# A transformer block in fp32: x also comes transposed from the host, and w_in's columns lie in the order of use

## The chip, the core and the metric

The kernel runs on one core of a Trainium2 chip. The metric is the device time of one execution in microseconds, as the median of several runs. The profile is of one execution, with the times of each engine's instructions: PE (TensorE, matmuls; PEld is its weight load), DVE (VectorE), ACT (ScalarE), POOL (GpSimd) and SP (SyncE, which here only issues DMAs). L361 means line 361 of the kernel.

## The reference, cut to what matters

One residual block on x of 256 tokens by 2048 channels, all in float32. A combined projection w_in (2048 x 5120) gives q, k and v of four attention heads and the two halves of a gated convolution branch; both results go through w_out, and a SwiGLU of width 5632 follows.

```python
xn = rms_norm(h, norm1_g[l])
proj = jnp.einsum('bsd,dn->bsn', xn, w_in[l].astype(xn.dtype))
q, k, v, ga, gg = jnp.split(proj, ..., axis=-1)
...
u = ga * jax.nn.sigmoid(gg)
u = causal_depthwise_conv(u, conv_w[l], conv_b[l])
u = jax.nn.silu(layer_norm(u, conv_ln_g[l], conv_ln_b[l]))
mixed = jnp.concatenate([att, u], axis=-1)
h = h + jnp.einsum('bsm,md->bsd', mixed, w_out[l].astype(mixed.dtype))
...
h = h + jnp.einsum('bsf,fd->bsd', jax.nn.silu(a) * bu, w_down[l].astype(hn.dtype))
```

## The kernel before, in words

**Products in three parts.** Each fp32 operand is split into a rounded part (hi) and the rest (lo), both in the fast fp32r format. A product is the sum of three matmuls: x_hi with w_hi (L361), x_lo with w_hi (L362) and x_hi with w_lo (L367). x is the stationary operand, a k-tile of 128 channels by 128 tokens; 512 columns of weights stream through. Each k-tile is therefore used in six matmuls, three for each of the two halves of the tokens.

**Chunks.** A matrix is worked off in blocks of 512 output columns, a block in chunks of two k-tiles, so that a chunk has 12 matmuls. `load_chunk` (L307) issues the chunk's weights on SP's DMA queue into one of five raw buffers (from the second block on, every third chunk goes to one of two spare buffers). `round_chunk` (L320) makes w_hi with a cast on ACT, L322. `split_chunk` (L328) makes w_lo with a subtraction on DVE, L331. `multiply` (L343) does the matmuls, first all with w_hi, then those with w_lo. `run_chunks` (L389) writes all of this down in one order: load, cast and split run ahead of the matmuls by one chunk in the opening (the first eight chunks) and by two after it. Each engine works through its instructions in that order.

**Steps beside the chunks.** Everything else is a generator that is resumed twice in each chunk, once between the two halves of the matmuls and once behind them (`resume`, L246). A `yield` puts the next step half a chunk later. The order on each engine is thus fixed by counts of chunks, not by time. The convolution's 240 taps on DVE (L512) are dealt out by a credit per k-tile (`run_side`, L272).

**The order of the work.** w_in comes first, in ten blocks: four for the convolution (each 256 columns of the gate and 256 of the value, thus two DMAs of 256 KB for a chunk), then k and q for two heads at a time, then v. Then come w_out, the gate and up matrices, and the down matrix. A block's sums lie in two PSUM banks, of four, until its finishing generator has read them: `glu_done` (L478) for the convolution, `qk_done` and `v_done` for the attention. `conv_back` (L526) takes the finished convolution through a layer norm: it transposes y to tokens (ps_y), makes its statistics on DVE (L543, L552) and POOL, normalises on ACT (L561), transposes back (ps_ln, L570), applies SiLU (z, L574) and splits into mchi and mclo (L577, L578), the operand of w_out's k-tiles 8 to 15.

**The opening before.** x comes with tokens on the partitions, in five pieces, each as two DMAs into the two tiles h (`x_load`, L432). Its k-tiles are transposed on PE (ps_x, L441), 32 transposes in all, and split from PSUM by ACT and DVE, scaled by the gain of the norm (`split_scaled`, L232; L235 and L236). The norm's factor rstd1 is applied to the block's sums later; its sum of squares comes from eight squares with an accumulated sum on ACT (L430), two reductions on DVE and four small POOL operations (L215). The gains come as rows and are transposed on PE (L157), and so are the convolution's weights (eight transposes, L184). 14 transposes of the identity at the start and five behind the first pieces of x keep PE busy (`warm_up`, L142).

Of the kernel before, what the change touches and what calls it, by code (L numbers as in the profile page):

```python
# [56 lines left out]
CONV_BLOCKS = (2, 2, 2, 2)  # L57
# [51 lines left out]

@with_exitstack  # L110
def tile_block(
    ctx: ExitStack,
    tc: tile.TileContext,
    x, w_in, conv_w, w_out, w_gate, w_up, w_down, gains, vecs, rope, out,
# [27 lines left out]
    def warm_up(n):  # L142
        warm = aux_ps.tile([P, N], F32, tag="aux", name="ps_warm")
        for _ in range(n):
            pe.transpose(warm[:, :P], ident, ident)

    warm_up(WARM[0])

    rows = pre.tile([NR, P], F32, tag="rows", name="rows", bufs=1)
    act.dma_start(out=rows, in_=gains)  # L150

    act.copy(small.tile([P, 8], F32, tag="rsq", name="first"), neghalf)
    cols = const.tile([P, NR], F32, tag="cols", name="cols")

    def gain_columns():
        ps = aux_ps.tile([P, N], F32, tag="aux", name="ps_cols")
        pe.transpose(ps[:, :NR], rows, ident[:NR, :NR])  # L157
        act.copy(cols, ps[:, :NR])
# [7 lines left out]
    cw_rows = [pre.tile([W, N], F32, tag="va", name="cw_rows") for _ in range(CC // N)]  # L166
# [4 lines left out]
    def late_loads():  # L171
        flat = conv_w.rearrange("o w i c -> (o w i) c")
        for i in range(CC // N):
            sp.dma_start(out=cw_rows[i], in_=flat[:, i * N : (i + 1) * N])
        for t, v in ((gb, vecs[:2]), (lamv, vecs[2:])):
            sp.dma_start(out=t, in_=v.rearrange("(o v) d -> o v d", o=1).to_broadcast(list(t.shape)))
        sp.dma_start(out=rt, in_=rope.rearrange("(m p) c d -> p m c d", p=P))

    def late_constants():
        late_loads()  # L180
        yield from lag(4)
        pw = aux_ps.tile([P, N], F32, tag="aux", name="ps_cw")
        for ct in range(NCT):
            pe.transpose(pw[:, ct * W : (ct + 1) * W], cw_rows[ct * P // N][:, ct * P % N : ct * P % N + P], ident[:W, :W])  # L184
        act.copy(cw.rearrange("p c w -> p (c w)"), pw[:, : NCT * W])
# [57 lines left out]
    def start(gen):  # L243
        running.append(gen)
# [45 lines left out]
    def block(w, cols, ks, xs, done=None, bkey=None, first=True, last=True, spare=False, cuts=()):  # L290
# [7 lines left out]
        while i < len(ks):  # L298
            part = ks[i : i + (cuts.pop(0) if cuts else NK * N // width)]
            i += len(part)  # L300
            chunks.append(dict(w=w, k0=part[0], nk=len(part), cols=cols, width=width, xs=xs, bkey=bkey,
# [124 lines left out]
    ss1 = [small.tile([P, D // N], F32, tag=f"ss1_{m}", name=f"ss1_{m}", bufs=1) for m in range(NM)]  # L426
# [4 lines left out]

    def x_load(ks):  # L432
        cs = slice(ks[0] * P, (ks[-1] + 1) * P)
        for m in range(NM):
            sp.dma_start(out=h[m][:, cs], in_=x[m * P : (m + 1) * P, cs])

    def x_part(ks):
        for k in ks:
            ps = aux_ps.tile([P, N], F32, tag="aux", name="ps_x")
            for m in range(NM):  # L440
                pe.transpose(ps[:, m * P : (m + 1) * P], h[m][:, k * P : (k + 1) * P], ident)  # L441
            xT[k] = lhs_pair("x", k)
            split_scaled(xT[k], ps[:, :S], col("g1", k))

    def x_rest():
        c = 0
        for part in XPARTS[1:]:
            while chunks_done[0] < (part[0] // NK) * 2 - 1:
                yield
            x_part(part)  # L450
            yield
            yield
            if part[-1] % (N // P) == N // P - 1:
                for m in range(NM):
                    square_sum(h[m][:, c * N : (c + 1) * N], ss1[m][:, c : c + 1])
                c += 1
        for m in range(NM):
            ss = small.tile([P, 1], F32, tag="ss1", name="ss1")
            dve.tensor_reduce(ss, ss1[m], AX.X, ALU.add)
            rsqrt_mean(rstd1[m], ss, D, EPS)  # L460
        yield
        normed.append(True)
# [122 lines left out]
    qkT = {key: pre.tile([P, 2 * H, S], F32, tag=f"{key}T", name=f"{key}T", bufs=1) for key in "qk"}  # L585

# [581 lines left out]
    QC, KC, VC, AC, GC = 0, 1024, 2048, 3072, 4096  # L1168
    fx, fh = xT.get, hT.get
    fm = lambda k: mixa.get(k) if k < 8 else mixc.get(k - 8)  # L1170
    c0 = 0
    for nct in CONV_BLOCKS:
        block(w_in, [(GC + c0 * P, nct * P), (AC + c0 * P, nct * P)], range(KD), fx,
              lambda ps, c0=c0, nct=nct: glu_done(c0, nct, ps))
        c0 += nct
    for b in range(2):
        block(w_in, KC + b * N, range(KD), fx, lambda ps, b=b: qk_done("k", b, ps))
        block(w_in, QC + b * N, range(KD), fx, lambda ps, b=b: qk_done("q", b, ps))
    for b in range(2):
        block(w_in, VC + b * N, range(KD), fx, lambda ps, b=b: v_done(b, ps))  # L1180
# [22 lines left out]
    for part in XPARTS:  # L1203
        before[part[0] // NK] = lambda part=part: x_load(part)
# [5 lines left out]
_FLAT = {"x": (S, D), "w_in": (D, 5120), "conv_w": (1, W, 1, CC), "w_out": (D, D), "w_gate": (D, FF),  # L1210
# [22 lines left out]
```

## Time and profile before

| | us |
|---|---|
| median of 3 runs (lowest to highest) | 1051.15 (1050.9 to 1052.19) |
| span of the profiled execution, first to last instruction | 1049.4 |
| PE busy in it | 1040.1 |
| DVE busy in it | 896.4 |
| ACT busy in it | 622.1 |

The profile gives the span of the profiled execution and no other time of that execution; the median of the runs lies 1.75 us above the span. The rows that the next part shows come from five views. The page's head has the busy time of each engine and its share of the span. A row of the stretches gives, for a window in us, the length, then for PE, PEld, DVE, ACT and POOL the busy time and the number of instructions, then the granted clock, the mean busy share of the 16 DMA engines and their GB/s. A row in order of time gives start and duration in us (of several instructions in a row, from the first's start to the last's end), engine, line, operation, what is written and read, and in brackets the engine's idle time before it and what ended that. The DMA view has one figure of GB/s for each fortieth of its window, and for an issue its size and the time to landing. The view of a tile sums up its instructions and the waits ahead of them.

### The profile page before, as it was taken

The numbers are of one execution on the slowest core, as the hardware profiler recorded it, in microseconds if no ns is written. First come the engines' busy times: TensorE is split into PE (matmuls) and PEld (weight loads), VectorE is DVE, ScalarE is ACT, GpSimd is POOL, SyncE is SP. The second block draws the span as 40 slices with busy tenths as digits, with TensorE's granted clock in tenths as the row PEclk, the third lists the DMA queues.
The fourth block names the chain that finished last, engine by engine and source line by source line (L and its number), as shares of the span: only waits on it lengthen the run. The fifth ranks groups of instructions, "written<-read, shape, count | busy, mean of one in ns | idle before, by whom it ended". The sixth has DMA issues, their size and how long they took to land.

```text
span 1049.4 us, 13104 instructions
## 1 busy us (share of the span) xinstructions
PE 1040.1 (99%) x4702; PEld 855.9 (82%) x4702; DVE 896.4 (85%) x1091; ACT 622.1 (59%) x798; POOL 99.3 (9%) x143
## 2 busy tenths in 40 slices
PE   8999999999999999999999999999999999999998
PEld 7888888877888788888888888888888888888886
DVE  4799989899675599999788898989978699989897
ACT  6645567756666565776453557666654447657442
POOL 0030022201100100000001000001000110010010
PEclk9999999999999999999999999999999999999999
DMA  9755555544446565988766789879757789798682
GB/s 297 238 180 199 186 176 180 176 158 148 168 155 231 190 233 204 260 271 255 217 224 175 226 262 272 254 217 292 244 182 240 201 221 290 222 290 263 187 266 86
DMA packets 122893, 229.22 MB, mean 218 GB/s; under 512 B 7892, under 2 KB 25742, under 8 KB 122828
## 3 DMA queue, kind: packets, MB, share of 16 engines
q1 hardware_dynamic: 113904, 201.61, 56.5%
q0 software_dynamic: 8864, 26.74, 13.3%
q8 instruction: 37, 0.61, 0.2%
q14 instruction: 28, 0.23, 0.1%
q10 hardware_dynamic: 60, 0.03, 0.0%
HBM read 202.14 MB, written 9.44 MB: 202 GB/s over the span
## 4 chain that ended last, share of the span: by engine, by line
PE 62%; DVE 2%; DMA 1%; ACT 0%; issue 0%; DVEq 0%
PE q L1017 12%; PE q L1011 12%; PE q L1012 12%; PE q L992 8%; PE q L990 8%; PE q L991 8%; PE ps_a L828 1%; DMA raw<-in_w_down_dram 1%; PE acc L367 1%; PE acc L361 1%; PE acc L362 1%; DVE wlo L331 1%; DVE wlt L973 0%; DVE wt L963 0%; ACT wh L969 0%
## 5 line engine op out<-in xcount | busy, mean ns | idle before, releaser
L322 ACT CAST whi<-raw 128x1024 fp32r<-128x1024 f32 x272 | 281.5, 1050 | 145.8 <-PE acc L362 56.8
L331 DVE TENSOR_TENSOR wlo<-raw,whi 128x1024 fp32r<-128x1024 f32 x238 | 288.3, 1224 | 82.2 <-ACT whi L322 82.1
L969 ACT CAST wh<-wt 128x2048 fp32r<-128x2048 f32 x52 | 99.5, 1914 | 78.7 <-DVE wt L965 78.3
L973 DVE TENSOR_TENSOR wlt<-wt,wh 128x2048 fp32r<-128x2048 f32 x52 | 119.1, 2290 | 14.7 <-ACT wh L969 14.5
L361 PE MATMUL acc<-whi,xhi 128*128 128x512 f32 x320 | 126.3, 395 | 1.0 <-ACT whi L322 0.9
L362 PE MATMUL acc<-whi,xlo 128*128 128x512 f32 x320 | 125.0, 391 | 0.5 <-DVE xlo L236 0.5
L1011 PE MATMUL q<-whi,chi 128*128 128x512 f32 x320 | 125.2, 391 | 0.0
L1012 PE MATMUL q<-whi,clo 128*128 128x512 f32 x320 | 124.6, 389 | 0.0
L990 PE MATMUL q<-wh,fhi 128*128 128x512 f32 x280 | 109.8, 392 | 0.0
L991 PE MATMUL q<-wh,flo 128*128 128x512 f32 x280 | 109.0, 389 | 0.0
L512 DVE SCALAR_TENSOR_TENSOR y<-upad,cw,y 128x256 f32<-128x256 f32 x240 | 102.5, 486 | 0.0
L1011 PE MATMUL q<-whi,ahi 128*128 128x512 f32 x256 | 100.2, 391 | 0.0
L1012 PE MATMUL q<-whi,alo 128*128 128x512 f32 x256 | 99.6, 389 | 0.0
L972 DVE TENSOR_TENSOR wlb<-wb,wh 128x1536 fp32r<-128x1536 f32 x52 | 91.1, 1752 | 1.8 <-ACT wh L966 1.8
L367 PE MATMUL acc<-wlo,xhi 128*128 128x512 f32 x320 | 87.7, 396 | 0.9 <-DVE wlo L331 0.8
L1017 PE MATMUL q<-wlo,chi 128*128 128x512 f32 x320 | 85.8, 390 | 0.0
L966 ACT CAST wh<-wb 128x1536 fp32r<-128x1536 f32 x52 | 76.7, 1474 | 0.0
L361 PEld LDWEIGHTS acc<-whi,xhi 128*128 128x128 f32 x320 | 60.1, 188 | 13.9 <-ACT whi L322 1.2
L362 PEld LDWEIGHTS acc<-whi,xlo 128*128 128x128 f32 x320 | 60.1, 188 | 13.5 <-DVE xlo L236 1.3
L1017 PEld LDWEIGHTS q<-wlo,chi 128*128 128x128 f32 x320 | 59.9, 188 | 13.1 <-DMA wlo<-raw 0.7
L367 PEld LDWEIGHTS acc<-wlo,xhi 128*128 128x128 f32 x320 | 59.3, 188 | 13.6 <-DVE wlo L331 1.8
L1012 PEld LDWEIGHTS q<-whi,clo 128*128 128x128 f32 x320 | 60.1, 188 | 12.3
(229 smaller groups left out, 1744.6 us busy)
## 6 DMA issues: line engine op xcount, KB each, us to landing
raw<-in_w_down_dram SPq DMA_DIRECT2D x64, 512.0 KB, 7.5
raw<-in_w_in_dram SPq DMA_DIRECT2D x48, 512.0 KB, 4.4
raw<-in_w_gate_dram SPq DMA_DIRECT2D x48, 512.0 KB, 6.9
raw<-in_w_up_dram SPq DMA_DIRECT2D x48, 512.0 KB, 6.2
wb<-in_w_up_dram SPq DMA_DIRECT2D x40, 512.0 KB, 3.8
wb<-in_w_gate_dram SPq DMA_DIRECT2D x40, 512.0 KB, 4.7
wlo<-raw POOLq DMA_DIRECT2D x34, 512.0 KB, 6.8
raw<-in_w_in_dram SPq DMA_DIRECT2D x64, 256.0 KB, 5.7
```

What stands on the lines that cost most here:

```text
L322: act.copy(c["hi"], c["raw"])
L331: dve.tensor_tensor(c["lo"], c["raw"], c["hi"].bitcast(F32), ALU.subtract)
L361: pe.matmul(ps[m], xhi[:, ms], hi[:, j, :], start=c["first"] and j == 0, stop=False)
L362: pe.matmul(ps[m], xlo[:, ms], hi[:, j, :], start=False, stop=False)
L367: pe.matmul(ps[m], xhi[:, ms], lo[:, j, :], start=False, stop=c["last"] and j == nk - 1)
L512: dve.scalar_tensor_tensor(y[:, ct, :], src, wk, y[:, ct, :], ALU.mult, ALU.add)
L973: dve.tensor_tensor(lot, c["t"], c["hi"][:, :SUMMED].bitcast(F32), ALU.subtract)
L990: pe.matmul(ps, hi, c["hi"][:, w], start=bool(first), stop=False)
L991: pe.matmul(ps, lo, c["hi"][:, w], start=False, stop=False)
L1011: pe.matmul(ps, xs[i][0][:, ms], hi[:, i, :], start=i == 0 and bool(c["first"].get(qs[m])), stop=False)
L1012: pe.matmul(ps, xs[i][1][:, ms], hi[:, i, :], start=False, stop=False)
L1017: pe.matmul(sum_bank(c, qs[m]), xs[i][0][:, ms], lo[:, i, :], start=False, stop=i == 1 and bool(c["last"].get(qs[m])))
```

## The change

- The host passes x a second time, transposed: `xt`, 128 channels by 16 k-tiles by 256 tokens. `x_load` brings it in five pieces (one, three, and three times four k-tiles), one DMA each, into the tiles that later hold q and k. `x_split` splits the k-tiles from SBUF; the 32 transposes go.
- The host orders w_in's columns as the blocks use them, so that every chunk is one DMA of 512 columns. It passes the gains as columns and the convolution's weights as 128 channels by 248, so that those nine transposes go too.
- The first two chunks of the first block have one k-tile each (256 KB of weights, six matmuls), so that the block has nine chunks, and the opening lasts nine.
- The sum of squares is made from the transposed x: four squares in place on ACT (128x1024), five additions on DVE, and two matmuls with a column of -0.5 for the sum over the channels (`x_norm`).
- Token-major x is loaded into h as two DMAs of 1 MB ahead of the load of chunk 40 (`x_whole`). It is wanted for the residual, behind w_out.
- The identity is transposed 17 times at the start, and no more after that.

```diff
-WARM = (14, 5)
-XPARTS = (range(0, 2), range(2, 4), range(4, 8), range(8, 12), range(12, 16))
-OPENING = KD // NK
+WARM = 17
+XLOADS = {0: range(0, 1), 1: range(1, 4), 3: range(4, 8), 5: range(8, 12), 7: range(12, 16)}
+XSQUARES = 4
+XWHOLE = 40
+FIRST_CUTS = (1, 1)
+OPENING = KD // NK + 1
...
+def w_in_columns():
+    q, k, v, a, g = (np.arange(1024) + 1024 * i for i in range(5))
+    c = CONV_TILES * P
+    conv = [part[i : i + c] for i in range(0, CC, c) for part in (g, a)]
+    return np.concatenate([*conv, k[:N], q[:N], k[N:], q[N:], v])
...
     def x_load(ks):
-        cs = slice(ks[0] * P, (ks[-1] + 1) * P)
-        for m in range(NM):
-            sp.dma_start(out=h[m][:, cs], in_=x[m * P : (m + 1) * P, cs])
-
-    def x_part(ks):
+        half = qkT["qk"[ks[0] // 8]]
+        sp.dma_start(out=half[:, ks[0] % 8 : ks[-1] % 8 + 1, :], in_=xt[:, ks[0] : ks[-1] + 1, :])
+
+    def x_split(ks):
         for k in ks:
-            ps = aux_ps.tile([P, N], F32, tag="aux", name="ps_x")
-            for m in range(NM):
-                pe.transpose(ps[:, m * P : (m + 1) * P], h[m][:, k * P : (k + 1) * P], ident)
             xT[k] = lhs_pair("x", k)
-            split_scaled(xT[k], ps[:, :S], col("g1", k))
+            split_scaled(xT[k], qkT["qk"[k // 8]][:, k % 8, :], col("g1", k))
...
+    def x_square(n):
+        part = lambda i: qkT["qk"[i // 2]][:, i % 2 * XSQUARES : (i % 2 + 1) * XSQUARES, :]
+        act.activation(part(n), part(n), AF.Square)
+        if n:
+            dve.tensor_tensor(part(0), part(0), part(n), ALU.add)
+
+    def x_norm():
+        for n in range(KD // XSQUARES):
+            while len(xT) < (n + 1) * XSQUARES:
                 yield
-            x_part(part)
-            yield
-            yield
...
+            x_square(n)
+            yield
+        sq = qkT["q"]
+        for w in (2, 1):
+            dve.tensor_tensor(sq[:, :w, :], sq[:, :w, :], sq[:, w : 2 * w, :], ALU.add)
+        yield from lag(2)
+        yield from room(1)
+        ps = aux_ps.tile([P, N], F32, tag="aux", name="ps_n")
+        for m in range(NM):
+            pe.matmul(ps[:, m : m + 1], sq[:, 0, m * P : (m + 1) * P], neghalf[:, :1], start=True, stop=True)
+        yield
+        ss = small.tile([P, NM], F32, tag="ss1", name="ss1")
+        act.copy(ss, ps[:, :NM])
+        for m in range(NM):
+            rsqrt_mean(rstd1[m], ss[:, m : m + 1], -D / 2, EPS)
         yield
         normed.append(True)
...
-    before[0] = lambda: (x_load(XPARTS[0]), gain_columns(), x_part(XPARTS[0]), warm_up(WARM[1]), start(x_rest()))
+    def opening(i):
+        def begin():
+            if i in XLOADS:
+                x_load(XLOADS[i])
+            x_split(chunks[i]["ks"])
+            if not i:
+                start(x_norm())
+        return begin
+
+    def x_whole():
+        for m in range(NM):
+            sp.dma_start(out=h[m], in_=x[m * P : (m + 1) * P, :])
+
+    for i in range(OPENING):
+        before[i] = opening(i)
     before[OPENING] = lambda: start(late_constants())
+    before[XWHOLE] = x_whole
```

More of the change, by code (lines that the diff above doesn't have):

```diff
@@ L113, in tile_block @@
     tc: tile.TileContext,
[L114 removed]
+    x, xt, w_in, conv_w, w_out, w_gate, w_up, w_down, gains, vecs, rope, out,
 ):
@@ L145, in warm_up @@
             pe.transpose(warm[:, :P], ident, ident)
-    warm_up(WARM[0])
-    rows = pre.tile([NR, P], F32, tag="rows", name="rows", bufs=1)
-    act.dma_start(out=rows, in_=gains)
+    warm_up(WARM)
+    cols = const.tile([P, NR], F32, tag="cols", name="cols")
+    act.dma_start(out=cols, in_=gains)
     act.copy(small.tile([P, 8], F32, tag="rsq", name="first"), neghalf)
[L153 to L158, printed above, removed]
     def col(key, k):
@@ L180, in late_constants @@
         late_loads()
[L181 to L185, printed above, removed]
         while not normed:
```

54 lines of the change are left out of this document (18 added, 36 removed).

## The prediction, made before the changed kernel ran

> **What bounds the kernel now.** I read the page first, then the stretches of the opening, the waits of the first 60 us, and the opening and the middle in order of time.
>
> ```profile
> span 1049.4 us, 13104 instructions
> PE 1040.1 (99%) x4702; PEld 855.9 (82%) x4702; DVE 896.4 (85%) x1091; ACT 622.1 (59%) x798; POOL 99.3 (9%) x143
> ```
> ```profile
> 5.00:10.00 5.00, 4.08 (x22) 3.44 (x22) 2.10 (x3) 2.99 (x6) 0.00 (x0) 1.00 0.88 261
> 10.00:15.00 5.00, 4.49 (x24) 3.45 (x23) 3.24 (x4) 3.06 (x9) 0.00 (x0) 1.00 1.07 368
> 15.00:20.00 5.00, 4.92 (x21) 3.49 (x20) 3.08 (x6) 4.75 (x11) 0.00 (x0) 1.00 1.08 359
> 60.00:80.00 20.00, 20.00 (x92) 16.58 (x91) 20.00 (x35) 9.77 (x15) 8.58 (x14) 1.00 0.60 184
> ```
> PE (first busy figure of a stretch) is the bound nearly everywhere. So a change pays only by taking instructions from PE or by filling PE's holes, and the holes lie before 20 us. The last two figures say why: from 10 to 20 us the DMA engines are full (1.07, 368 GB/s), while at 60 us they are 0.60 busy.
>
> ```profile
> 1.35 3.25 PE L145 MATMUL ps_warm<-ident 128*128 128x128 f32 x14 [1.35 <-POOL neghalf L139]
> 5.72 0.83 PE L145 MATMUL ps_warm<-ident 128*128 128x128 f32 x5
> 6.38 1.04 ACT L322 CAST whi<-raw 128x1024 fp32r<-128x1024 f32 x1
> 7.48 0.50 PE L361 MATMUL acc<-whi,xhi 128*128 128x512 f32 x1 [0.93 <-ACT whi L322]
> 8.05 0.40 PE L361 MATMUL acc<-whi,xhi 128*128 128x512 f32 x1
> 9.21 0.40 PE L362 MATMUL acc<-whi,xlo 128*128 128x512 f32 x1
> 12.65 1.05 ACT L322 CAST whi<-raw 128x1024 fp32r<-128x1024 f32 x1 [1.91 <-DMA raw<-in_w_in_dram]
> 22.24 0.39 PE L361 MATMUL acc<-whi,xhi 128*128 128x512 f32 x1
> 24.96 0.39 PE L361 MATMUL acc<-whi,xhi 128*128 128x512 f32 x1
> 26.78 1.03 PE L441 MATMUL ps_x<-ident,h 128*128 128x128 f32 x8
> 34.02 0.39 PE L361 MATMUL acc<-whi,xhi 128*128 128x512 f32 x1
> ```
> The real work starts at 7.48. A chunk (two k-tiles, 12 matmuls) without additions takes 24.96 - 22.24 = 2.72 us. The first block has eight chunks, 21.8 us of matmuls, and the second block starts at 34.02: 26.5 us after the first matmul. The 4.8 us over are the transposes of x within the block (28 of them, at 1.03/8 = 0.13 us at most 3.6 us) and waits (1.2 us or more).
>
> **The change, part by part.**
>
> *The opening.* What arrives when, by one row (GB/s in slices of 1 us from 0 to 40):
>
> ```profile
> GB/s 0 29 243 270 333 195 226 343 254 289 360 377 364 381 357 348 356 368 370 353 348 356 311 302 291 331 226 305 183 151 56 327 337 276 287 300 330 339 366 348
> raw<-in_w_in_dram SPq DMA_DIRECT2D x38, 256.0 KB, 5.8
> ```
> Before, the first cast needs two k-tiles of x and of weights, 768 KB, which the running sum of the row reaches at 4.7 us; the cast starts at 6.38, so landing and semaphore add 1.65 us. After, the first cast needs 128 KB of x and 256 KB of weights: reached at 3.45, cast at 5.1. For a 128x512 cast I take 0.62 us, just above the 0.59 of the ACT copy of that size below. First matmul: 5.7 us instead of 7.48. The 17 transposes in a row end earlier: 3.25 us for 14, so 3.9 us for 17, done at 5.3.
>
> ```profile
> 40.97 0.59 ACT L501 COPY upad<-ps_u 128x512 f32<-128x512 f32 x1 [1.25 <-PE ps_u L500]
> 27.20 1.57 ACT L235 ACTIVATE xhi<-ps_x,cols 128x256 fp32r<-128x256 f32 x4 [1.51 <-PE ps_x L441]
> 27.71 1.66 DVE L236 SCALAR_TENSOR_TENSOR xlo<-ps_x,cols,xhi 128x256 fp32r<-128x256 f32 x4 [0.76 <-ACT xhi L235]
> 29.74 1.23 DVE L331 TENSOR_TENSOR wlo<-raw,whi 128x1024 fp32r<-128x1024 f32 x1 [0.37 <-ACT whi L322]
> ```
> Chunks 0 and 1 (one k-tile, 1.36 us each) and chunk 2 could be done at 5.7 + 5.44 = 11.15. The next one (k-tiles 4 and 5) decides. Ahead of its cast stand 2560 KB, exactly what stood ahead of the cast at 12.65 before; by that pace its first matmul comes at 12.65 + 1.05 + 0.05 = 13.75. The other end is 11.15, with PE alone. Between them stands ACT: the weights of chunk 2 (1536 KB so far) land at 8.3 by the best pace of the row (370 kB per us) with the 1.65 us behind it, and at 9.4 by the old pace. Then follow a cast of 1.05, the new squares of four k-tiles (128x1024; I take the cast of that size, 1.05), two x casts (0.8) and a cast of 1.05: 12.3 to 13.4. I take 12.6, nearer the fast end: a load of a conv chunk is now one DMA of 512 KB and not two of 256 KB, so whatever number of DMAs is in flight carries more bytes, and at 5 to 7 us the row dips to 195 and 226 though more loads were ready to go.
>
> From there six chunks of 2.72 lead to the second block: 12.6 + 16.3 = 28.9, against 34.02. **Term A: -5.1 us**, ends -6.6 (PE alone, 27.45) and -3.95 (old pace, 30.05). It contains the 28 transposes, the stalls and the earlier start. DVE must keep up: from 12.4 us on it has six wlo (1.23), five pairs of x splits (0.83), three new sums of 128x1024 (1.23), and two short ones (some 1.1 together): 7.4 + 4.2 + 3.7 + 1.1 = 16.4 us, done at 28.8. That is just in time for the two norm matmuls, which stand at 28.9; this cover has nothing to spare. Splitting from SBUF instead of PSUM I cost at 0: the duration could only differ by part of a 0.42 us instruction.
>
> *Gains and conv weights.* Both now come in the order in which they are used.
>
> ```profile
> 4.53 0.36 PE L157 MATMUL ps_cols<-ident,rows 58*128 58x58 f32 x1
> 38.64 0.68 PE L184 MATMUL ps_cw<-ident,cw_rows 31*128 31x31 f32 x8
> ```
> The gain transpose lay ahead of the first matmul (in A). The eight conv transposes stood in PE's full stream: **B: -0.7 us**. The Trainium skill (DMA: Bandwidth & Descriptors, Specifications) asks for at least 512 B per piece; the gains' rows are now 232 B. Before, the gains were there by 4.53 without a wait of PE, and no row prices such short ones.
>
> *The norm.* Two fp32 matmuls with one column replace nothing on PE: between nothing and the 0.36 us of the 58-column one, each. **C: +0.35 us** for both (0.1 to 0.7). The eight squares and reads on ACT and two reductions on DVE go; four squares and five sums come, counted above. rstd1 is ready two to three chunks later than before, but the sums of a block stay in one of two pairs of PSUM banks until the next block but one starts, eight chunks on.
>
> *The conv branch.* This is the cost I would not have seen in the diff. Block one has nine chunks, and the norm's steps are tied to chunks, so the first taps stand half a chunk to a chunk later in the order on DVE, and so does everything behind the last tap. In the built order of PE, the transposes of y for the second half move from matmul 1044 to 1052, and those of the normalised y from 1092, 1100, 1104, 1112 to 1100, 1104, 1112, 1116 (counted in 512-column matmuls). The w_out matmuls that read the result stay at 1104. Before, this chain had little slack:
>
> ```profile
> 280.06 0.33 DVE L552 BATCH_NORM_AGGREGATE mv<-stats 128x2 f32<-128x12 f32 x2
> 282.80 0.19 POOL L557 TENSOR_SCALAR lnb<-lnb 128x2 f32<-128x2 f32 x1
> 285.39 1.52 ACT L561 ACTIVATE upad<-upad,lnb,lnr 128x512 f32<-128x512 f32 x2
> 286.82 1.00 ACT L574 ACTIVATE z<-ps_ln,cols 128x256 f32<-128x256 f32 x2
> 287.72 0.43 DVE L578 TENSOR_TENSOR mclo<-z,mchi 128x256 fp32r<-128x256 f32 x1
> 288.79 1.23 DVE L331 TENSOR_TENSOR wlo<-raw,whi 128x1024 fp32r<-128x1024 f32 x1
> 289.78 0.40 PE L362 MATMUL acc<-whi,mclo 128*128 128x512 f32 x1
> ```
> mclo is done at 288.15 and first read at 289.78: 1.6 us to spare. After, the aggregate stands behind one more weight split and ends 1.85 us later against PE's stream; z stands behind the same casts, and one wlo (1.23, of which 0.8 counts) comes ahead of mchi on DVE: mclo is some 2.75 us later, while PE arrives 0.4 us earlier, since one group of transposes now stands behind these matmuls. 2.75 + 0.4 - 1.6: **D: +1.5 us**, ends 0 (the 1.6 us of slack plus the two POOL steps running shorter) and 2.4.
>
> *Token-major x at chunk 40.* 2 MB more on SP's queue between two weight loads.
>
> ```profile
> DMA to landing us min/median/max: 3.6/4.5/5.9
>   PE acc L362: 15.9, 10
> ```
> This is the view of the weight loads from 95 to 130 us: they land at most 5.9 us after the issue, and the casts wait for PE (10 times) and never for a DMA. Of seven raw buffers, a load goes out some four to five chunks before its cast, 11 to 13.6 us. The 2 MB take 2.1/0.37 = 5.7 us, less than what is left, and the cast itself runs two chunks ahead of its matmuls. Cost 0; without that cover see below. The 2 MB are wanted only by the residual, after 290 us.
>
> **Sum:** -5.1 - 0.7 + 0.35 + 1.5 = -3.95 us. The profiled span of 1049.4 becomes 1045.45. The median of the runs lies 1.75 us above that span; I leave this as it is: 1051.15 - 3.95 = **1047.2 us**.
>
> **The rivals.**
> 1. *More is won:* the loads keep up (A -6.3) and the conv chain fits (D 0): 1044.9. For it: fewer, larger DMAs; against it: ACT's chain above.
> 2. *The feed stays as slow as before*, so the earlier start turns into waits for DMA: A is -3.95, 1048.4. This is also how the small first chunks would fail to do what they are for: at 12.65 the old kernel had received just as many bytes. Against it: the DMA engines were not full from 5 to 10 us (0.88).
> 3. *The clock.* The 14 transposes run at 0.23 us each, the later ones at 0.13, and the first real matmuls already at their full pace (8.05 to 9.21 is five, 0.23 each). So PE's pace doubled within the second group of transposes, some 4.6 us after its first instruction, though the granted clock of the stretches stands at 1.00. If the longer gap without real matmuls, or transposes alone, do not bring that about, the first matmuls run at half pace for 4.6 us: of 24 matmuls in chunks 0 to 2 some 10 are done at 10.3, the rest at 13.5, 0.9 us behind 12.6: 1048.1. The Trainium skill (TensorE: Matmul & The Clock Gate, Part 4: PE-mode transpose) says that transposes do not count as busy for the clock; by that rule this case would hold. The trace disagrees: the pace doubled with nothing but transposes issued.
> 4. *Slower than before:* the 2 MB of x hold up the weights. If the loads behind them land later than their casts are due and the two chunks of lead are used up, PE stands for as long as x takes: at 300 kB per us, 7 us, giving 1054.2. It decides once the delay exceeds the 5 to 8 us left before the cast and the 4 us after it. Against it: DMA is 0.60 busy there.
>
> **How the numbers follow.** The forecast has 0.55, rival 1 0.18, rival 2 0.12, rival 3 0.05, rival 4 0.06; 0.04 is left for an opening on DVE that does not fit. The range joins the ends: -6.6 - 0.7 + 0.1 + 0 = -7.2 gives 1044.0; -3.95 - 0.6 + 0.7 + 2.4 = -1.45 gives 1049.7. A measurement of this kernel can tell some 0.2%, 2.1 us, from no change: faster means below 1049.05. The forecast and rivals 1 to 3 lie there but for their upper ends: faster 0.85, same 0.08, slower 0.07.
>
> **What would show it.** First matmul at 5.7 (5.2 to 6.5), the first of chunk 3 near 12.6, the second block at 28.9. No wait of the norm matmuls over 0.3 us. One wait of PE for mclo or mchi of 1 to 2 us where w_out's second half starts, 4 us earlier than 289. No wait of a cast for a DMA around 100 to 125 us. I am wrong if the second block starts after 31 us, or if stalls that the change does not touch (the attention between 210 and 265 us) move by more than 1 us.

## The result, and the profile after

| | before | after |
|---|---|---|
| median of 14 runs each, us | 1051.12 (1050.71 to 1052.41) | 1049.12 (1048.44 to 1049.90) |
| span of the profiled execution, us | 1049.4 | 1047.1 |

The ratio is 0.9979, 95% interval 0.9971 to 0.9987: 2.0 us faster, and inside the range that was given (1044.0 to 1049.7). The interval excludes 1, but the prediction called a result faster only below 1049.05, and 1049.12 is just above that line. The forecast was 1047.2; half of the gain that it counted on did not arrive. The opening won nearly what it should. Some 2.3 us were taken back in three places behind it, of which the prediction had named one.

The page of the changed kernel, and its stretches (length; busy time and count of PE, PEld, DVE, ACT, POOL; granted clock; DMA share; GB/s):

```profile
span 1047.1 us, 12933 instructions
PE 1036.2 (99%) x4663; PEld 852.5 (81%) x4663; DVE 900.6 (86%) x1095; ACT 621.6 (59%) x786; POOL 100.5 (10%) x143
...
5.00:10.00 5.00, 4.05 (x14) 2.74 (x12) 2.32 (x5) 2.71 (x5) 0.00 (x0) 1.00 0.93 337
10.00:15.00 5.00, 4.91 (x22) 3.94 (x22) 4.20 (x7) 4.67 (x9) 0.00 (x0) 1.00 1.05 399
15.00:20.00 5.00, 5.00 (x24) 4.14 (x23) 5.00 (x8) 4.51 (x7) 0.00 (x0) 1.00 1.05 392
```

PE has 39 instructions fewer. The feed from 5 to 20 us is faster than before (337, 399 and 392 GB/s against 261, 368 and 359), and from 15 us on PE is busy without a hole. The opening in order of time, changed kernel:

```profile
1.36 3.89 PE L157 MATMUL ps_warm<-ident 128*128 128x128 f32 x17 [1.36 <-POOL neghalf L151]
4.89 0.78 PE L359 MATMUL acc<-whi,xhi 128*128 128x512 f32 x1
5.47 0.63 PE L360 MATMUL acc<-whi,xlo 128*128 128x512 f32 x1
5.89 0.63 PE L359 MATMUL acc<-whi,xhi 128*128 128x512 f32 x1
...
7.16 0.51 ACT L233 ACTIVATE xhi<-qT,cols 128x256 fp32r<-128x256 f32 x1 [2.54 <-DMA qT<-in_xt_dram]
8.47 0.50 PE L359 MATMUL acc<-whi,xhi 128*128 128x512 f32 x1 [0.95 <-ACT whi L320]
...
13.06 0.39 PE L359 MATMUL acc<-whi,xhi 128*128 128x512 f32 x1
...
29.39 0.50 PE L460 MATMUL ps_n<-neghalf,qT 128*128 128x1 f32 x4
29.75 0.49 PE L359 MATMUL acc<-whi,xhi 128*128 128x512 f32 x1
```

The first matmul comes at 4.89, but the second chunk stands until 8.47: ACT waits until 7.16 for the piece of x with k-tiles 1 to 3, and its cast of the second chunk's weights stands behind that. Chunk 3 (k-tiles 4 and 5) starts at 13.06, and from there six chunks run at 2.72 us each up to the norm's matmuls at 29.39, which wait for nothing and take 0.36 us (29.75 - 29.39).

Where the lead goes is seen by setting the same work side by side. Counted are the 512-column matmuls of the blocks, in groups of twelve; the table has the start of a group in both traces.

| start of | before | after | lead |
|---|---|---|---|
| first matmul | 7.48 | 4.89 | 2.59 |
| group 8 (second block) | 34.02 | 29.75 | 4.27 |
| group 11 | 43.54 | 38.52 | 5.02 |
| group 55 (q and k) | 166.82 | 161.85 | 4.97 |
| group 56 | 170.03 | 166.14 | 3.89 |
| group 72 | 220.42 | 216.78 | 3.64 |
| group 90 (w_out) | 282.74 | 279.12 | 3.62 |
| group 93 | 292.77 | 290.11 | 2.66 |
| end of the span | 1049.4 | 1047.1 | 2.3 |

So 1.08 us are lost within one group of q and k, 0.25 in two groups near 214 us, 0.96 where w_out's second half begins, and 0.36 behind it. The first of these, in the changed kernel (POOL, DVE, ACT and PE in order of time):

```profile
143.11 1.09 ACT L543 COPY upad<-ps_y 128x512 f32<-128x512 f32 x2
...
148.00 0.42 POOL L217 TENSOR_SCALAR rsq<-ssq 128x4 f32<-128x4 f32 x1 [19.74 <-ACT junk L427]
148.50 3.40 POOL L218 TENSOR_TENSOR fq<-rsq,neghalf 128x4 f32<-128x4 f32 x1
148.68 2.35 DVE L329 TENSOR_TENSOR wlo<-raw,whi 128x1024 fp32r<-128x1024 f32 x2
152.31 1.14 ACT L619 ACTIVATE qn<-acc,fq 128x128 f32<-128x128 f32 x4 [1.61 <-POOL fq L615]
154.42 1.23 DVE L329 TENSOR_TENSOR wlo<-raw,whi 128x1024 fp32r<-128x1024 f32 x1 [3.39 <-ACT whi L320]
...
164.74 1.20 PE L365 MATMUL acc<-wlo,xhi 128*128 128x512 f32 x4 [0.80 <-DVE wlo L329]
```

and the same chain before:

```profile
152.39 0.19 POOL L219 TENSOR_SCALAR rsq<-ssq 128x4 f32<-128x4 f32 x1 [19.16 <-ACT junk L430]
...
154.08 2.23 POOL L612 TENSOR_SCALAR fq<-fq,rstd 128x4 f32<-128x4 f32 x1
156.34 1.14 ACT L616 ACTIVATE qn<-acc,fq 128x128 f32<-128x128 f32 x4 [1.26 <-POOL fq L612]
```

Before, ACT starts qn when the factors fq are there, at 156.34, which less the lead of 4.97 is 151.37; after, at 152.31. It is 0.94 us late, ACT's next weight casts stand behind it, DVE idles for 3.39 us (2.28 before), and ten microseconds later PE waits for a wlo. A POOL step on four columns that takes 3.40 us is the odd row here, but it is not the larger part. POOL has such a row in both traces (3.40 after, 2.23 before), and its steps up to fq take 4.28 us after (148.00 to 152.28) and 3.92 before (152.39 to 156.31): 0.36 us more. The other 0.58 us are there when POOL starts (148.00, against 152.39 - 4.97 = 147.42), because ACT's squares end later: the two copies of ps_y at 143.11 now stand directly ahead of two weight casts and the squares, while before they stood at 144.95, ahead of 1.58 us in which ACT was idle. On DVE one tap more (0.39 us) stands ahead of the wlo for which PE waits. The three add up to the 1.33 us by which that wlo is late against the lead (its subtraction starts at 163.47, before at 167.11 - 4.97 = 162.14). That the order of the steps is behind them is shown by e1 and e2.

The third loss, at w_out's second half in the changed kernel:

```profile
279.71 1.07 POOL L562 TENSOR_SCALAR lnb<-lnb 128x2 f32<-128x2 f32 x1
280.81 2.94 ACT L566 ACTIVATE upad<-upad,lnb,lnr 128x512 f32<-128x512 f32 x4 [1.34 <-POOL lnb L562]
...
286.20 0.50 PE L359 MATMUL acc<-whi,mchi 128*128 128x512 f32 x1 [0.58 <-DVE mchi L582]
```

This is the wait for mchi that the prediction named; the first matmul with mclo follows 0.46 us later. Before, the same POOL step took 0.19 us, but there the first step of the same chain took 1.20 us.

### The profile page after: what moved, and what is told of

It is laid out like the page before. It is cut to its first block, busy times and chain, and to the rows that moved or that the text cites. A ratio compares the mean times of both kernels' runs of the same rounds, so it can differ in the third digit from the quotient of the medians.

```text
span 1047.1 us, 12933 instructions
## 1 busy us (share of the span) xinstructions
PE 1036.2 (99%) x4663; PEld 852.5 (81%) x4663; DVE 900.6 (86%) x1095; ACT 621.6 (59%) x786; POOL 100.5 (10%) x143
## 4 chain that ended last, share of the span: by engine, by line
PE 61%; DMA 2%; DVE 2%; issue 1%; ACT 0%; DVEq 0%; POOLq 0%
PE q L1020 12%; PE q L1014 12%; PE q L1015 12%; PE q L995 8%; PE q L993 7%; PE q L994 7%; DMA raw<-in_w_down_dram 1%; PE ps_a L831 1%; DMA wlo<-raw 1%; PE acc L365 1%; PE acc L359 1%; PE acc L360 1%; DVE wlo L329 1%; DVE wlt L976 0%; DVE wt L966 0%
## 5 line engine op out<-in xcount | busy, mean ns | idle before, releaser
L320 ACT CAST whi<-raw 128x1024 fp32r<-128x1024 f32 (+1 forms) x273 | 281.5, 1048 | 141.6 <-PE acc L360 58.9
L329 DVE TENSOR_TENSOR wlo<-raw,whi 128x1024 fp32r<-128x1024 f32 (+1 forms) x239 | 287.8, 1218 | 73.5 <-ACT whi L320 73.3
L1014 PEld LDWEIGHTS q<-whi,chi 128*128 128x128 f32 x320 | 60.1, 188 | 12.3
```

The source lines that it names most:

```text
L320: act.copy(c["hi"], c["raw"])
L329: dve.tensor_tensor(c["lo"], c["raw"], c["hi"].bitcast(F32), ALU.subtract)
L1014: pe.matmul(ps, xs[i][0][:, ms], hi[:, i, :], start=i == 0 and bool(c["first"].get(qs[m])), stop=False)
```

## The experiments

The theory at this point: the opening won about 5 us; the conv chain standing half a chunk to a chunk later on DVE makes all three later waits. The rivals: the opening is held by the size of x's pieces, or the later waits have another cause. Of the numbers below, "opening" means the start of the matmuls of k-tiles 4 and 5 and of the second block. Every run was timed beside the kernel before; ratios are to it. None of the twelve kernels leaves out any part of the computation.

**e1: the norm half a chunk earlier** (in `x_norm` of the changed kernel)

```diff
-        yield from lag(2)
+        yield from lag(1)
```

> The changed kernel with the norm's two matmuls half a chunk earlier (one resume less of waiting in x_norm). In the built order this puts the first taps, the y transposes and the transposes of the normalised y back at the places they had in the old kernel (120, 564 and 1044, 1092 to 1112). If the order is what costs the changed kernel its time behind the opening (theory: order), the wait of PE for wlo at 163.6 us (1.0 us) and the one for mchi at 286.2 (0.6, with mclo some 1.0) go, and nothing else moves: the span falls from 1047.1 by 2.0 to 1045.1, the median to about 1047.0, ratio to the old kernel 0.996. If the two waits are chance, of POOL and DVE running in another phase after the shorter opening (theory: phase), the first one stays and the ratio is 0.997 or above. The norm matmuls then stand at about 28.5 us, the sums on DVE are done at 28.6: a wait of at most 0.3 us.

Measured: 1047.62 us (5 runs), ratio 0.9967 (0.9954 to 0.9979). The wait at 163.6 and those for mchi and mclo are gone. But two new ones stand in the second block (view in order of time, e1):

```profile
28.49 0.58 PE L460 MATMUL ps_n<-neghalf,qT 128*128 128x1 f32 x4
...
36.17 0.94 PE L505 MATMUL ps_u<-ident,u 128*128 128x128 f32 x4 [0.61 <-DVE u L497]
```

PE now reaches the transposes of u 0.6 us before DVE has made u, and the norm's matmuls stand in the middle of a chunk, ahead of its wlo. So the order decides, as the theory has it (it said 1047.0). Pulling the whole of it forward costs 1.18 us of lead in the second block (3.84 at group 11, against 5.02), half of the 2.29 us that it saves later.

**e2: the kernel before, with the norm's end delayed by as much**

```diff
         yield
+        yield from lag(4)
         normed.append(True)
```

> The old kernel with four resumes more before the norm counts as done, which puts the first taps and all that follows at the places of the changed kernel (128, 572 and 1052, 1100 to 1116) and leaves the opening as it was. Theory order: it becomes slower by the 2.0 us that the changed kernel loses behind its opening, median 1053.1, ratio 1.002, with a wait for wlo some 4 us later than 163.6 and one for mchi. Theory phase: no change but the second wait at most, ratio 1.000 to 1.001.

Measured: 1053.82 us (8 runs), ratio 1.0024 (1.0013 to 1.0034). The old kernel, with its old opening and x transposed on the chip, now has the same waits, in the same places and of the same size (PE in order of time, e2):

```profile
169.97 1.19 PE L367 MATMUL acc<-wlo,xhi 128*128 128x512 f32 x4 [0.79 <-DVE wlo L331]
...
291.39 0.49 PE L361 MATMUL acc<-whi,mchi 128*128 128x512 f32 x1 [0.58 <-DVE mchi L578]
```

The two idle times of the changed kernel were 0.80 and 0.58. Counted by the same groups, e2 falls behind the kernel before by 1.04, 0.27 and 0.97 us, where the changed kernel lost 1.08, 0.25 and 0.96. That the three losses come from the shifted order, and not from x, w_in or the loads, is shown by this run together with e1.

**e3: k-tile 1 of x by itself**

```diff
-XLOADS = {0: range(0, 1), 1: range(1, 4), 3: range(4, 8), 5: range(8, 12), 7: range(12, 16)}
+XLOADS = {0: range(0, 1), 1: range(1, 2), 2: range(2, 4), 3: range(4, 8), 5: range(8, 12), 7: range(12, 16)}
```

> The changed kernel with x in six loads: k-tile 1 alone ahead of the weights of chunk 1, k-tiles 2 and 3 behind them. In the changed kernel chunk 1 waits 1.3 us for the load of k-tiles 1 to 3 (384 KB, landed at 7.1), and runs at 8.47. Theory feed: 256 KB less stand ahead of it, so chunk 1 starts 0.7 to 1.0 us earlier, and so does all that follows: second block at 29.0 instead of 29.75, ratio 0.9972. Theory ACT: chunk 2 is set by the cast of its weights and the splits on ACT, chunk 1 starts earlier and the second block does not: ratio 0.998 as before.

Measured: 1048.72 us (11 runs), ratio 0.9979 (0.9970 to 0.9988), that of the changed kernel. The second chunk no longer waits for x (it starts at 6.75 instead of 8.47), and nothing comes of it. ACT and PE in order of time, e3:

```profile
8.65 1.04 ACT L320 CAST whi<-raw 128x1024 fp32r<-128x1024 f32 x1 [0.75 <-DMA raw<-in_w_in_dram]
11.90 1.05 ACT L320 CAST whi<-raw 128x1024 fp32r<-128x1024 f32 x1 [0.45 <-PE acc L360]
13.00 0.50 PE L359 MATMUL acc<-whi,xhi 128*128 128x512 f32 x1 [0.22 <-ACT whi L320]
```

ACT's wait moved on to the weights of the next chunk, and then to a whi buffer that PE had not yet freed; k-tiles 4 and 5 start at 13.00. The time in which the second chunk stands in the changed kernel lies beside loads and casts that set the start of chunk 3 anyway.

**e4: the kernel before, with w_in's columns in the order of use**

```diff
-        block(w_in, [(GC + c0 * P, nct * P), (AC + c0 * P, nct * P)], range(KD), fx,
+        block(w_in, c0 // 2 * N, range(KD), fx,
...
+    given["w_in"] = given["w_in"][:, w_in_columns()]
```

> The old kernel with w_in's columns in the order of use alone: each chunk is one DMA of 512 KB with rows of 2 KB instead of two of 256 KB with rows of 1 KB. Theory feed: the opening was held up by the loads (casts waited 6.2 us for them), so the waits of PE within the first block (1.2 us or more) and part of the wait ahead of it shrink: second block 1 to 1.5 us earlier than 34.02, ratio 0.9988. Theory transposes: what the change gained in the opening was the transposes and the smaller first chunks, and the feed matters little: ratio 0.9995 to 1.

Measured: 1051.04 us (11 runs), ratio 1.0002 (0.9993 to 1.0011). The first matmul comes later and the second block when it did (PE in order of time, e4; 34.02 before):

```profile
8.34 0.50 PE L369 MATMUL acc<-whi,xhi 128*128 128x512 f32 x1 [1.35 <-ACT whi L330]
...
33.91 0.39 PE L369 MATMUL acc<-whi,xhi 128*128 128x512 f32 x1
```

With the transposes still in the stream, larger loads alone win nothing.

**e5: only the first taps half a chunk earlier**

```diff
         act.copy(upad[c0 // NB][:, c0 % NB : c0 % NB + nct, W - 1 :], pt[:, :nct])
-        yield
+        if c0:
+            yield
```

> The changed kernel with one difference: for the first block's conv chunk the pause between copying u into upad and starting the taps is dropped, so that the norm and the transposes of u stay where the change put them (96 and 128 in 512-column matmuls) while the taps, and the transposes of y (564, 1044) and of the normalised y (1092, 1100, 1104, 1112) behind them, go back to the old places. Nothing is left out. Theory (the later order of the taps alone makes the late waits): the waits at 163.6 us (1.19), at the start of w_out's second half (0.85 and 0.46) and the 0.4 more at 214 go, and the waits at ps_n and ps_u that the kernel with the norm moved had (0.49 and 1.00) do not come: 2.3 us below the changed kernel, 1046.8 us, ratio about 0.996. Rival (the late waits come from where the norm stands, not from the taps): they stay, 1049.1, ratio 0.998. Rival (the time given back comes out elsewhere, as with the moved norm): 1047.7.

Measured: 1047.46 us (5 runs), ratio 0.9961 (0.9949 to 0.9974). The waits for mchi and mclo are gone, as in e1, and the new waits of e1 do not come. But a wait near 164 is still there (1.39 us of lead go between groups 53 and 56), and the time lies between the theory's 1046.8 and the 1047.7 of time given back: the place of the taps alone does not explain this wait, and the theory falls for it. In order of time, e5:

```profile
149.68 3.49 DVE L329 TENSOR_TENSOR wlo<-raw,whi 128x1024 fp32r<-128x1024 f32 x3
149.70 4.79 POOL L217 TENSOR_SCALAR rsq<-ssq 128x4 f32<-128x4 f32 x1 [0.28 <-ACT junk L427]
153.08 0.68 DVE L627 TENSOR_TENSOR t<-qn,gcsq 128x512 f32<-128x512 f32 x1
...
154.02 0.42 DVE L629 TENSOR_TENSOR t<-qn,gcsq 128x256 f32<-128x256 f32 x1
156.44 1.14 ACT L620 ACTIVATE qn<-acc,fq 128x128 f32<-128x128 f32 x4 [4.85 <-POOL fq L616]
...
164.54 1.21 PE L365 MATMUL acc<-wlo,xhi 128*128 128x512 f32 x4 [0.63 <-DVE wlo L329]
```

A POOL step on four columns begins with the first of six DVE instructions that each read two tensors of SBUF and follow each other without a break, and ends at 154.49, when the sixth ends (154.44). The Trainium skill (SBUF — State Buffer, Who interferes with whom) says that a VectorE instruction with two SBUF inputs contends with a GpSimd instruction that reads SBUF; the row agrees, and adds that the hold lasts over a whole row of such instructions. The new theory: where the POOL steps of the q/k norm and of the conv branch's deviation fall against DVE's weight subtractions decides what they take. A shift of half a chunk changes that too. The rival: POOL is slow there for a reason of its own.

**e6: no short first chunks**

```diff
-XLOADS = {0: range(0, 1), 1: range(1, 4), 3: range(4, 8), 5: range(8, 12), 7: range(12, 16)}
-XWHOLE = 40
-FIRST_CUTS = (1, 1)
-OPENING = KD // NK + 1
+XLOADS = {0: range(0, 2), 1: range(2, 4), 2: range(4, 8), 4: range(8, 12), 6: range(12, 16)}
+XWHOLE = 39
+FIRST_CUTS = ()
+OPENING = KD // NK
```

> The changed kernel without its two short first chunks: all chunks of the first block have two k-tiles, x comes in pieces of 2, 2, 4, 4, 4 k-tiles, everything else and the order behind the first block as in the changed kernel (taps late). Nothing is left out. Theory (ACT's chain of casts and squares and the feed set when k-tiles 4 and 5 start, near 13.0 us, and the short chunks only fill PE's holes ahead of that): first matmul near 6.5 instead of 4.9, k-tiles 4 and 5 start between 12.5 and 13.5, second block within 0.5 us of 29.75; time within 0.6 us of the changed kernel, 1048.6 to 1049.7. Rival (the short chunks bring the earlier start themselves): everything behind is later by the 1.5 us of the first matmul: 1050.6.

Measured: 1047.98 us (5 runs), ratio 0.9969 (0.9956 to 0.9981), below what either theory said (1048.6 or more), with an interval that overlaps that of the changed kernel. PE in order of time, e6:

```profile
6.87 0.50 PE L359 MATMUL acc<-whi,xhi 128*128 128x512 f32 x1 [1.62 <-ACT whi L320]
...
12.69 0.40 PE L359 MATMUL acc<-whi,xhi 128*128 128x512 f32 x1
```

The first matmul is 2 us later, k-tiles 4 and 5 are 0.4 us earlier. That is within the spread: in e1, e5, e7 and e8, whose instructions up to there are those of the changed kernel, k-tiles 4 and 5 start between 12.57 and 13.06. The short chunks bring the first matmul forward and nothing behind it; that they cost something is not shown.

**e7: the mean's product on ACT**

```diff
-        pool.tensor_tensor(lnb, mv[:, :, 0], lnr, ALU.mult)
-        pool.tensor_scalar(lnb, lnb, -1.0, 0.0, ALU.mult, ALU.add)
         yield from lag(2)
+        for m in range(NM):
+            act.activation(lnb[:, m : m + 1], mv[:, m, 0:1], AF.Copy, scale=lnr[:, m : m + 1])
+        act.activation(lnb, lnb, AF.Copy, scale=-1.0)
```

> The changed kernel with the two small products of the conv branch's mean and deviation (lnb, 2 columns) on ACT, behind the pause and directly ahead of the normalisation that reads them, instead of on POOL. Nothing is left out. Theory (the second of the POOL products, 1.07 us beside a wlo subtraction on DVE and 0.19 without one, holds ACT up: it waited 1.34 us for lnb): ACT goes on 0.4 to 0.8 us earlier, and of the two waits at the start of w_out's second half (0.85 and 0.46 us) 0.4 to 0.8 go: 1048.5, ratio to before 0.9974. Rival (the chain is late by the order of DVE alone): the normalisation starts where it did, 280.8, and the waits stay: 1049.1. The wait at 163.6 us stays in both.

Measured: 1047.99 us (5 runs, 1048.5 was expected), ratio 0.9966 (0.9954 to 0.9979). In order of time, e7:

```profile
280.11 2.94 ACT L567 ACTIVATE upad<-upad,lnb,lnr 128x512 f32<-128x512 f32 x4
...
285.50 0.49 PE L359 MATMUL acc<-whi,mchi 128*128 128x512 f32 x1
```

The normalisation starts at 280.11 instead of 280.81, and the wait for mchi is gone (285.50 instead of 286.20). So 0.7 us of the loss at w_out go when the last two steps leave POOL. That the stretch of one of them is what the changed kernel lost is not shown by this: POOL's four steps took 2.41 us in the changed kernel (278.37 to 280.78) and 2.52 before (280.47 to 282.99). What is late is their start, by 1.52 us against the lead of 3.62, and e5, which changes the order alone, has the whole loss back.

**e8: e5 and e7 together**

```diff
-        yield
+        if c0:
+            yield
...
-        pool.tensor_scalar(lnb, lnb, -1.0, 0.0, ALU.mult, ALU.add)
...
+        act.activation(lnb, lnb, AF.Copy, scale=-1.0)
```

> The changed kernel with both of the above: the taps of the first block start half a chunk earlier, and lnb is made on ACT. Nothing is left out. If the two act on the same waits, this gains nothing over the earlier taps alone: 1046.8, ratio 0.996. If they add up: 1046.3. If the earlier products only shift ACT's casts, 1047 or more.

Measured: 1047.46 us (5 runs), ratio 0.9961 (0.9948 to 0.9975): the same as e5. The two act on the same wait.

**e9: e5, with a break on DVE behind each weight subtraction**

```diff
+    gap = const.tile([P, 1], F32, tag="gap", name="gap")
...
             dve.tensor_tensor(c["lo"], c["raw"], c["hi"].bitcast(F32), ALU.subtract)
+            dve.memset(gap, 0.0)
```

> The kernel of e5 (taps half a chunk earlier) with one tiny DVE instruction (a memset of one column, no tensor input) behind every wlo subtraction. Nothing is left out. In e5 a POOL step of the q/k norm of four columns took 4.79 us, beside three wlo subtractions and three further DVE instructions with two SBUF inputs in an unbroken row (0.19 us is the shortest for the same step), and ACT waited 4.85 us for it; PE then waited 1.02 us for wlo at 163.5. Theory (POOL is held while DVE works through two-input instructions without a break): the break lets POOL in behind the first wlo, the step takes at most 1.3 us, and the waits at 158.1 (0.5) and 163.5 (1.0) go: 1046.1, ratio 0.9947. Rival (POOL gets in only when DVE stands still, or the step is long for another reason): 4.8 us and the waits as in e5, 1047.5, or up to 0.3 more for the memsets.

Measured: 1046.56 us (5 runs), ratio 0.9955 (0.9942 to 0.9967), the lowest median of all kernels here, though the interval overlaps those of e5 and e11. POOL and DVE in order of time, e9:

```profile
150.28 1.30 POOL L218 TENSOR_SCALAR rsq<-ssq 128x4 f32<-128x4 f32 x1 [0.23 <-ACT junk L429]
150.30 2.36 DVE L330 TENSOR_TENSOR wlo<-raw,whi 128x1024 fp32r<-128x1024 f32 x2
151.47 0.06 DVE L331 MEMSET gap<- 128x1 f32 x1
151.66 1.88 POOL L219 TENSOR_TENSOR fq<-rsq,neghalf 128x4 f32<-128x4 f32 x1
```

A break of 0.06 us takes the step from 4.79 to 1.30 us: it ends at 151.58, one subtraction after it began. The waits at 158 and 163.5 are gone, and one of two at 210 to 214. The rival would have left 4.8 us. From group 53 to group 56, where e5 loses 1.39 us of lead, e9 loses none. Behind w_out the profiled execution does not keep all of it: its lead is 5.37 us where the matmuls of the SwiGLU begin (388.1) and 4.01 at the end, while e5's goes from 3.81 to 3.69. Between 598 and 613 the weight loads of PE wait 0.7 us for a wlt of DVE (0.2 in e5). Whether the 239 memsets cause any of this is not shown.

**e10: the changed kernel with w_in's columns in their old order**

```diff
-        block(w_in, i * N, range(KD), fx, d, cuts=() if i else FIRST_CUTS)
+        block(w_in, where[i], range(KD), fx, d, cuts=() if i else FIRST_CUTS)
...
-    given["w_in"] = given["w_in"][:, w_in_columns()]
```

Here `where[i]` holds the old columns: for a conv block two ranges of 256, loaded by two DMAs.

> The changed kernel with w_in's columns in their old order: each conv chunk's weights come as two DMAs (gate and value columns) instead of one, everything else as in the changed kernel. Nothing is left out. Theory (what is won in the opening comes from the transposes and splits that left, not from the order of the columns): first matmul within 0.4 us of 4.9, k-tiles 4 and 5 within 0.4 us of 13.06, time within 0.6 us of the changed kernel, 1048.5 to 1049.7. Rival (one DMA of 512 KB instead of two of 256 KB is what makes the feed keep up): k-tiles 4 and 5 start near 13.75 or later, 1049.8 or more.

Measured: 1049.70 us (11 runs), ratio 0.9986 (0.9977 to 0.9995). In order of time, e10:

```profile
5.42 0.62 ACT L320 CAST whi<-raw 128x512 fp32r<-128x512 f32 x1 [1.66 <-DMA raw<-in_w_in_dram]
...
13.63 0.50 PE L359 MATMUL acc<-whi,xhi 128*128 128x512 f32 x1 [0.22 <-ACT whi L320]
```

The first weights are there 1.4 us later (5.42 against 4.01), k-tiles 4 and 5 start 0.57 us later, and the second block at 30.45 instead of 29.75. So the order of columns is worth 0.6 to 0.7 us of the opening against this one execution of the changed kernel, once the transposes are gone (13.63 lies 0.57 to 1.06 us behind the 12.57 to 13.06 of the five kernels that share its opening); the result lies between the two expectations. The intervals of the times overlap with the changed kernel's, so this rests on the traces.

**e11: e5 without short chunks, and e12: with the break as well.** The edits are those of e5 and e6, and in e12 of e9 too:

```diff
-FIRST_CUTS = (1, 1)
+FIRST_CUTS = ()
...
+            dve.memset(gap, 0.0)
```

> The kernel of e5 (taps half a chunk earlier) with the opening of e6 (no short first chunks). Nothing is left out. Theory (the short chunks gain nothing, the taps gain what e5 gained): within 0.5 us of e5, 1047.0 to 1048.0, ratio 0.996. Rival (both gains add up, the short chunks cost 1 us as the medians alone would say): 1046.4, ratio 0.9954.

> The kernel of e11 (taps half a chunk earlier, no short first chunks) with the tiny DVE instruction of e9 behind every wlo subtraction. Nothing is left out. If the three act on different waits, as their traces say (e9 took the waits at 158 and 163.5 and some of those at 210 to 215 from e5, and the opening of e11 led by 0.9 us in the profile): 1046.1, ratio 0.995, second block near 29.1, no wait over 0.4 us at 158 to 166. Rival (what the opening of e11 wins is lost again in waits behind it): as e9, 1046.6 or more.

Measured: e11, as expected, 1047.04 us (5 runs), ratio 0.9964 (0.9952 to 0.9977); e12 1047.54 us (5 runs, 1046.17 to 1049.07), ratio 0.9963 (0.9949 to 0.9977). The time of e12 is the rival's, but not by waits behind the opening: those at 158 to 166 are gone as in e9. In the profiled execution (1048.49 us) it is the opening itself, the worst of all the variants of the changed kernel. PE in order of time, e11:

```profile
1.35 3.52 PE L157 MATMUL ps_warm<-ident 128*128 128x128 f32 x17 [1.35 <-POOL neghalf L151]
...
6.81 0.39 PE L360 MATMUL acc<-whi,xlo 128*128 128x512 f32 x1
7.04 0.40 PE L359 MATMUL acc<-whi,xhi 128*128 128x512 f32 x1
```

and e12:

```profile
7.54 0.63 PE L362 MATMUL acc<-whi,xlo 128*128 128x512 f32 x1
7.97 0.63 PE L361 MATMUL acc<-whi,xhi 128*128 128x512 f32 x1
...
12.66 0.49 PE L362 MATMUL acc<-whi,xlo 128*128 128x512 f32 x1
```

One matmul every 0.23 us in e11 (6.81 to 7.04), one every 0.43 us (7.54 to 7.97) in e12, until 12.7 us: the rival of the clock, in full, and at 3.1 us (second block at 31.97 against 28.85) dearer than the 0.9 us that the prediction gave it. Both traces have 17 transposes and then a pause of PE; in e11 the transposes had already sped up by themselves (3.52 us for 17, against 3.89). The times of e11 and e12 spread more than those of e9 (1046.8 to 1048.6 and 1046.2 to 1049.1, against 1046.1 to 1047.2). That the slow opening of some executions makes this spread fits, but only the profiled executions show it. The version to keep is e9, by its median and its trace; the intervals do not tell it from e5 and e11.

## Why the prediction was right in its sign and too large in its size

- **Term A, the opening** (-5.1, measured -4.6: the lead of 4.27 at group 8 and the 0.36 of the norm's matmuls). The bound was named rightly: what decides is the start of chunk 3, not the first matmul. It was set at 12.6 and came at 13.06, which is the whole difference, since the six chunks after it took 16.33 us (29.39 - 13.06) where 16.3 was said; the same opening gave 12.57 in e5, so 12.6 is within what executions differ by. The first matmul was said to come at 5.7 (5.2 to 6.5) and came at 4.89, outside, and it did not matter (e3, e6). The step "one DMA of 512 KB and not two of 256 KB" held (e10), worth 0.6 to 0.7 us. The column order alone is worth nothing in the old kernel (e4) and the short chunks nothing in the new one (e6): what remains for the rest of A is x that comes transposed, with its loads; this is by elimination, since the change cannot be made with the transposes kept.
- **Term B** (-0.7) and **term C** (+0.35): between groups 8 and 11 the lead grows by 0.75; the norm's matmuls took 0.36.
- **Token-major x** (0): the lead is 5.02 at group 11 and 4.97 at group 55, with the 2 MB between. In the waits of ACT from 94 to 130 us no cast waits for a DMA (changed kernel; engine, what is waited for, total, times, longest):

```profile
ACT whi L320 <- PE acc L360: 14.2, 9, 1.7
```

- **Term D, the conv branch** (+1.5 at the start of w_out's second half, measured +0.96): the wait and its place were right, and in the main the way to it: the aggregate was said to end 1.85 us later against PE's stream and ends 1.51 later (278.28, against 280.39 - 3.62 = 276.77). The help by "the two POOL steps running shorter" did not come: the first ran 0.19 us instead of 1.20, but the last ran 1.07 instead of 0.19.
- **The step that failed:** "everything behind the last tap". The shift was followed along one path only, from the taps to mclo. The same half chunk moves the first half's ps_y copies on ACT, the POOL steps and the taps among the weight casts and subtractions while q and k are normed: +1.08 in group 55 and +0.25 near 214, which the sum does not have. e1 and e2 show that the order makes these losses; the rows divide the first into ACT (0.58 of the 1.33 us by which the wlo is late), one tap more on DVE (0.39) and a longer hold of POOL (0.36). No run tests these three apart in the changed kernel, and the 0.25 is not divided. In e5, where the taps are back in their place, the wait near 164 has another cause, a POOL step caught for 4.79 us, and there e9 takes it away with a break of 0.06 us. The prediction's own warning sign was set for the stalls "between 210 and 265" and did not look at 163. That POOL's steps can be caught was to be seen in the trace of before: the 2.23 us of the q/k step shown above, and a first POOL step of 1.20 us at the deviation.
- **Luck:** D was set 0.5 us too high, which made up for part of the 1.33 us that the sum lacks. Rival 1's own terms add up to -6.3 - 0.7 + 0.35 = -6.65, thus 1044.5 and not 1044.9; nothing hangs on it.
- **Rival 3, the clock:** it came in part, and cost nothing. The first chunk of the changed kernel runs at 0.42 us per matmul (5.47 to 5.89), and the second waits for x until 8.47 anyway. The Trainium skill's rule that transposes do not count as busy (TensorE: Matmul & The Clock Gate, Part 4: PE-mode transpose) is borne out by e12 and contradicted by e11, whose transposes sped up with nothing else issued; the runs do not settle what sets the moment.
- **What adds up:** -4.63 - 0.75 + 0.36 + 1.08 + 0.25 + 0.96 = -2.73, and 0.4 more lie behind group 93: 0.1 up to the end of w_out, and 0.5 near 422 us, where a matmul of the changed kernel waits for a wlo that a DMA makes (idle 0.25 us at 422.36), of which some 0.3 come back by 674. Why that DMA is later is open. The span fell by 2.3, the median by 2.0.

## What to carry to other kernels

A gain in the opening of a kernel whose order is tied to chunks is also a shift of everything that hangs on the order: set the same work of both traces side by side by count, and look for each place where the lead shrinks, not only for the one that was foreseen. When a small step on POOL takes several times its shortest row, look at what DVE does in the same microseconds; a break between DVE's two-input instructions can let it in (4.79 to 1.30 us from e5 to e9). But compare the same chain in the trace of before as well: here POOL was held there too, and most of the delay came from elsewhere. Of several changes made at once to bring the first instruction forward, the first instruction's start says little: look for the first load or cast that is on the path, and time the start of the work behind it.

## What the runs showed of the hardware that had not been expected

- POOL's small steps stretch beside DVE: the same step (`rsq` on four columns) took 0.19 us alone, 1.30 beside one subtraction and 4.79 beside six two-input DVE instructions in a row; `lnb` on two columns took 0.19 or 1.07 us.
- PE's pace in the first microseconds is not the same from one execution to the next, under a granted clock of 1.00 throughout: it doubled during the transposes in e11, near 7 us in the changed kernel and only near 12.7 us in e12.
